# Pinning mixer products behind conditioning visits, and moving the conditioning loads to another queue

## The chip, the cores and the metric

The kernel runs on one NeuronCore of a Trainium2 chip. The metric is device time in microseconds of one execution, as the median of several runs. The engines are named as in the profile: PE is TensorE's matmul, PEld its weight load, DVE is VectorE, ACT is ScalarE, POOL is GpSimd, SP is SyncE, which here only issues DMAs.

## The reference, cut to what matters

One inference step of a decoder layer for 256 prompt tokens and 8 x 4 sample tokens (288 columns in all), width 2048, all in 32-bit floats:

```python
mod = silu(c) @ w_ada + b_ada                       # conditioning: 6 vectors of 2048 for 9 sequences
sh1, sc1, gt1, sh2, sc2, gt2 = split(mod, 6)
xn = rmsnorm(x, g_norm1) * (1 + sc1) + sh1
proj = xn @ w_in                                    # q, k, v, gates of three recurrent branches
y_lru, y_gla, y_ml = rglru(...), gla(...), mlstm(...)   # each also returns its updated state
merged = sum(sigmoid(mg[b]) * (y[b] @ w_br[b]) for b in range(3))
x = x + gt1 * (merged @ w_out)
xn = rmsnorm(x, g_norm2) * (1 + sc2) + sh2
x = x + gt2 * (square(relu(xn @ w_ff1)) @ w_ff2)
y = rmsnorm(x, g_final)
```

The weights are read once: 410 MB come from HBM by the page. The sample group's GLA and mLSTM states (8 and 16 blocks of half a megabyte) are read, updated and written back.

## The kernel before, in words

**The stream.** Activations lie feature-major: 128 partitions by 288 columns for each of 16 tiles of features. `stream` (line 148) multiplies one block of 512 output features: for each group of two k-tiles it loads 512 KB of weights (`raw`, line 155, on SyncE's queue), rounds them to a high part on ScalarE (line 156), takes the low part on VectorE (line 158), and issues 24 matmuls (line 165: high x high, high x low, low x high; four feature tiles, two k-tiles). `raw`, `hi` and `lo` have three buffers each. A block has 8 groups when it sums over 2048 features and 4 when it sums over 1024. After the last group an eviction reads the four PSUM tiles. The order of the blocks is: three q, k, v blocks in two halves of k each (`NPRE = 3`), the fourth of these, two LRU blocks, two GLA gate blocks, the merge of the LRU branch (four times a gate block and a block of `w_br`), two mLSTM input blocks, the GLA merge, two output-gate blocks, the mLSTM merge, `w_out`, then the MLP.

**The steps.** `run` (line 191) drives a block. After each group it does one letter of a pattern set by `every`: `L` starts the next conditioning load, `V` is a visit, `.` nothing. Then it advances each generator in `side` by one step. The generators are the rest of the work, cut into steps by `yield`: the normalisation, `lru`, `gla`, `gates`, `mlstm`. `pace` keeps the last instruction of some kinds: `last` the last matmul of the stream, `hi` and `lo` the last rounding and difference of weights, `prod` the last conditioning product. `skip` in `every` counts the groups before the pattern starts.

**Conditioning.** `w_ada` is 100 MB, and its products have only 9 columns on one side. They are cut into units of at most 1 MB of weights (`units`, `cond_product`). A load puts a unit into a tile given by `raw_tile` from a rotating list of slots that are free at that stage: `None` is the ring tile "ag", a number is one of the big slots, "st" is the pair of tiles that also holds GLA and mLSTM states. A visit multiplies all loaded units (line 269), with the vector as the stationary operand, in strips of 32 columns of the array.

**What sets the order.** A scheduler orders the instructions of every engine by priority and readiness; SyncE alone keeps program order (`manual_schedule`). `issue_after(x)` puts what is traced inside it behind instruction x on x's engine; it is an order, not a wait for the end. Side steps are traced with high priority behind `last`, `lo` and `hi`; a `V` is traced with high priority behind `last`, ahead of the side step of the same group.

**Lines that matter.** `add_slot` (514) adds the second half of a q, k, v block to the first (517) and multiplies by rstd (518). `conv_tile` (587, its taps at 591) and `conv` (593) are the causal convolutions, one or two of eight tiles a step; their sample part runs on GpSimd (601 to 615). In `gla`, `tile_` reads a state tile with the query (1004) and updates it, `head` (1023) scales a head's output, states are loaded at 989 and stored at 1051. In `mlstm`, states are loaded at 1389 (`mC`), read at 1405, updated at 1425 and stored at 1430. Evictions of the merges are at 1099 to 1103. The merges are driven by `merge` (1071).

Of the kernel before, what the change touches and what calls it, by code (L numbers as in the profile page):

```python
# [11 lines left out]
ALU = mybir.AluOpType  # L12
AX = mybir.AxisListType

P = 128
# [6 lines left out]
N = NP + NS  # L22
# [30 lines left out]
def trunk(ctx, tc, io):  # L53
    nc = tc.nc
    PSUM = bass.MemoryType.PSUM
    V, S, G, T, Q = nc.vector, nc.scalar, nc.gpsimd, nc.tensor, nc.sync
# [130 lines left out]
    def every(p, skip=0):  # L187

        pace.update(every=p.split(), n=-skip)

    def run(gen):
        for _ in gen:
            if pace["every"]:
                if pace["n"] >= 0:
                    step(pace["every"][pace["n"] % len(pace["every"])])
                pace["n"] += 1
            for g in list(side):
                with tc.high_priority(), ExitStack() as behind:
                    for e in ("last", "lo", "hi"):
                        behind.enter_context(tc.issue_after(pace[e].ins))  # L200
                    if next(g, side) is side:
                        side.remove(g)
# [4 lines left out]
    def beside(g):  # L207
        side.append(g)
        return g

    def finish(g):

        while g in side:
            if next(g, side) is side:
                side.remove(g)
# [16 lines left out]
        V.transpose(t, ps[:, 256 * h:256 * h + n])  # L232
        return t.rearrange("p (m c) -> p m c", c=32)

    slots = {"ids": (None,), "n": 1}
    halves_of = {}

    def raw_tile():
# [58 lines left out]
    wada = io["wada"]  # L297
# [4 lines left out]
    def ada(kind):  # L302
        def load(raw, k):
            if len(raw) == 2:
                for h in range(2):
                    Q.dma_start(raw[h], wada[kind, h, k])
            else:
                Q.dma_start(raw[0].rearrange("p (h m) -> p h m", h=2), wada[kind, :, k].rearrange("h p m -> p h m"))
        return cond_product(kind, load, 1, 2048, silu_c, ada_finish(kind))

    def ada_half(name, kind, h):

        def load(raw, q):
            Q.dma_start(raw[0].rearrange("p (k m) -> p k m", k=2), wada[kind, h, 2 * q:2 * q + 2].rearrange("k p m -> p k m"))
        return cond_product(name, load, 2, 1024, silu_c, lambda _, pv: ada_finish(kind)(h, pv))

    def shift_product(dst, nb):

        def load(raw, k):
            Q.dma_start(raw[0][:, 0:512 * nb].rearrange("p (b m) -> p b m", b=nb),  # L320
                        io["win"][B_Q:B_Q + nb, k // 2, :, 512 * (k % 2):512 * (k % 2) + 512].rearrange("b p m -> p b m"))

        def add(h, o):
            n = o.shape[1]
            while h and shifts[0] in side:
                yield
            for m in range(n):
                d = dst[h][:, m, 0:NP]
                V.tensor_scalar(d, d, o[:, m, 0:1], None, ALU.add)
                yield  # L330
            d = smp(dst[h])[:, 0:n]
            G.tensor_tensor(out=d, in0=d, in1=o[:, :, 1:9].unsqueeze(3).to_broadcast([P, n, NB, TS]), op=ALU.add)

        def end(h, pv):
            o = sc([P, 8, 9], "cor")[:, 0:pv.shape[1]]
            V.tensor_copy(o, pv[:, :, 0:9])
            shifts.append(beside(add(h, o)))
        return cond_product("cor", load, 1, 512 * nb, lambda k: modf[:, (SH1 * KT + k) * 9:(SH1 * KT + k) * 9 + 32], end)
# [124 lines left out]
    qk, vv = slot(8), slot(9)  # L463
# [50 lines left out]
    def add_slot(dst, base):  # L514
        def f(m, p):
            d = dst[:, base + m, :]
            V.tensor_tensor(out=d, in0=d, in1=p, op=ALU.add)
            V.tensor_tensor(out=d, in0=d, in1=rs, op=ALU.mult)
        return f

    def more_x():
        i = len(xs_)
# [41 lines left out]
    ssq, rs = row("rr"), row("lf")  # L564
# [11 lines left out]
    for h in range(2):  # L576
        for b in range(NPRE):
            ev = (add_slot if h else to_slot)((qk, vv)[b // 2], 4 * (b % 2))
            run(stream(win, B_Q + b, act1, 8 + 8 * h, ev, k0=8 * h, behind=None if h or b else ready))
    finish(pre)  # L580
    every("L L L L . V")
    slots.update(ids=(5, 6, 7, None, 0, 3), n=0)
    rest = beside(last_shifts())
    for b in range(NPRE, 4):
        run(stream(win, B_Q + b, act1, KT, to_slot((qk, vv)[b // 2], 4 * (b % 2))))
# [7 lines left out]
    def conv(x, y, w, b, state, cout, scr, tiles=range(8)):  # L593

        w = w.rearrange("p (k j) -> p k j", k=8)
        f = flat(scr)
        xp = f[:, 0:448].rearrange("p (k b j) -> p k b j", k=8, b=NB)
        acc = f[:, 448:704].rearrange("p (k b t) -> p k b t", k=8, b=NB)
        tmp = f[:, 704:960].rearrange("p (k b t) -> p k b t", k=8, b=NB)
        co = f[:, 960:1176].rearrange("p (k j) -> p k j", k=8)  # L600
        G.dma_start(f[:, 1176:1368], io[state])
        G.tensor_copy(xp[:, :, :, 3:7], smp(x))
        G.tensor_copy(xp[:, :, :, 0:3], f[:, 1176:1368].rearrange("p (k b j) -> p k b j", k=8, b=NB))
        bc = [P, 8, NB, TS]
        for j in range(4):
            wj = w[:, :, j:j + 1].unsqueeze(3).to_broadcast(bc)
            if j == 0:
                G.tensor_tensor(out=acc, in0=xp[:, :, :, 0:4], in1=wj, op=ALU.mult)
                G.tensor_tensor(out=acc, in0=acc, in1=b.unsqueeze(2).unsqueeze(3).to_broadcast(bc), op=ALU.add)
            else:  # L610
                G.tensor_tensor(out=tmp, in0=xp[:, :, :, j:j + 4], in1=wj, op=ALU.mult)
                G.tensor_tensor(out=smp(y) if j == 3 else acc, in0=acc, in1=tmp, op=ALU.add)
        G.tensor_copy(co[:, :, 0:3], x[:, :, NP - 3:NP])
        G.tensor_copy(co[:, :, 3:27].rearrange("p k (b j) -> p k b j", b=NB), xp[:, :, :, 4:7])
        G.dma_start(io[cout], co)
        for m in tiles:
            conv_tile(x, y, w, b, m)
            if len(tiles) < 8 or m not in (0, 3):
                yield


    def lru():
# [101 lines left out]
    with tc.high_priority(), tc.issue_after(pace["prod"].ins):  # L724
        p = misc()
# [110 lines left out]
    def gla():  # L836
# [7 lines left out]
        for h in range(4):  # L844
            p = misc()
# [37 lines left out]
        for t in range(2):  # L883
            for q in range(2):
                p = misc()
# [5 lines left out]
        p = misc()  # L891
# [5 lines left out]
        p = misc()  # L897
# [25 lines left out]
        for t in range(2):  # L923
            p = misc()
# [107 lines left out]
        def do(s, f, *a):  # L1032
            at.setdefault(s, []).append(lambda: f(*a))
# [11 lines left out]
        for h in range(4):  # L1045
            e = 6 * h + (9 if h < 3 else 7)
            do(e, lambda h: gather_tokens(oT, h, pos.pop(h)), h)
            do(e + 1, head, h)
        for n in range(8):
            do(3 + 3 * n, tile_, n)  # L1050
            do(4 + 3 * n, lambda n: S.dma_start(io["o_gla_s"][n], tiles[n][:, 0:1024]), n)
# [19 lines left out]
    def merge(br, y, w):  # L1071
        for b in range(4):
            if br == 0 and b == 2:
                visit()
                slots.update(ids=(None,), n=0)
                every("L . V . . .", skip=5)
            if br == 0:
                gt = acc[b // 2][:, 4 * (b % 2):4 * (b % 2) + 4, :]
            elif br == 1:
                gt = ring.tile([P, 2048], F32, tag="ag", name=nm("ag"))[:, 0:4 * N].rearrange("p (k n) -> p k n", k=4)  # L1080
            else:
                gt = slot(4)[:, 0:4, :]
            run(stream(win, B_MG + 4 * br + b, act1, KT, lambda m, p: S.activation(gt[:, m, :], p, AF.Tanh, scale=0.5)))

            if br == 0 and b == 0:
                for g in (*shifts, lru_):
                    finish(g)
                gla_.append(beside(gla()))
            if br == 1 and b == 0:
                finish(gla_[0])  # L1090
            if br == 2 and b == 0:
                finish(ml_)
                mrg.extend([slot(0, F32R), slot(1, F32R), slot(2, F32R), slot(3, F32R)])

            def ev(m, p):
                k = 4 * b + m
                a = acc[k // 8][:, k % 8, :]
                if br == 0:
                    V.scalar_tensor_tensor(a, gt[:, m, :], 1.0, p, ALU.add, ALU.mult)
                    return  # L1100
                t = t288()
                V.scalar_tensor_tensor(t, gt[:, m, :], 1.0, p, ALU.add, ALU.mult)  # L1102
                (V if br == 1 else G).tensor_tensor(out=a, in0=a, in1=t, op=ALU.add)  # L1103
                if br == 2:
                    h, l = mrg[k // 8][:, k % 8, :], mrg[2 + k // 8][:, k % 8, :]
                    S.activation(h, a, AF.Copy, scale=0.5)
                    V.scalar_tensor_tensor(l, a, 0.5, h.bitcast(F32), ALU.mult, ALU.subtract)

            run(stream(w, b, lambda k: (y[0][:, k, :], y[1][:, k, :]), 8, ev))
# [394 lines left out]

    merge(1, ygla, io["wbg"])
    slots.update(ids=(None, 8), n=0)
    every("L L . V . . .", skip=5)

    mo = slot(3)
    for b in range(2):  # L1510
# [63 lines left out]
    rs = rstd_of(pss)  # L1574
# [190 lines left out]
```

## Time and profile before

| | |
|---|---|
| median of 3 runs | 1971.24 us (1967.84 to 1971.85) |
| the profiled execution | 1971.56 us, its span 1969.5 us |
| PE busy | 1931.1 us, 98% of the span |
| DVE, ACT, POOL busy | 52%, 42%, 10% |
| mean granted clock of TensorE | 0.996 |
| DMA | 429 MB, 218 GB/s on average |

The page has the busy time of the engines, the span in 40 slices, the DMA queues, the chain of waits that ended last, and the costliest groups of instructions. A row of a group reads: line, engine, operation, output tile and input tiles, shapes, count, then busy time and the mean of one in ns, then the engine's idle time ahead of these instructions and what ended it. A row of the timeline reads: start, length, engine, line, operation, tiles, shapes, count, and in brackets the idle time before it with what ended it. A row of the waits reads: who waited for whom, total us, times, longest. Matmul ends are modelled, so the distance between starts says more than the busy time. A conditioning product shows as two records.

### The profile page before, as it was taken

The numbers are of one execution on the slowest core, as the hardware profiler recorded it, in microseconds if no ns is written. First come the engines' busy times: TensorE is split into PE (matmuls) and PEld (weight loads), VectorE is DVE, ScalarE is ACT, GpSimd is POOL, SyncE is SP. The second block draws the span as 40 slices with busy tenths as digits, with TensorE's granted clock in tenths as the row PEclk, the third lists the DMA queues.
The fourth block names the chain that finished last, engine by engine and source line by source line (L and its number), as shares of the span: only waits on it lengthen the run. The fifth ranks groups of instructions, "written<-read, shape, count | busy, mean of one in ns | idle before, by whom it ended". The sixth has DMA issues, their size and how long they took to land.

```text
span 1969.5 us, 35874 instructions
## 1 busy us (share of the span) xinstructions
PE 1931.1 (98%) x15044; PEld 1820.2 (92%) x15044; DVE 1026.1 (52%) x1576; ACT 823.9 (42%) x1179; POOL 206.4 (10%) x279
## 2 busy tenths in 40 slices
PE   6999999999999999999999999999999999999997
PEld 4889889899899999899999899999999999999997
DVE  2573536545674457654445564445444445444565
ACT  3433364435454354343333454443333334343433
POOL 0000100000014010001113331000000000010101
PEclk9999999999999999999999999999999999999999
DMA  9998757547754459967788655644445544444453
GB/s 384 407 342 300 273 207 265 177 139 248 253 169 139 135 186 319 299 248 268 266 290 333 210 192 183 225 161 161 163 162 176 171 164 161 161 162 168 162 173 113
DMA packets 119378, 429.00 MB, mean 218 GB/s; under 512 B 11745, under 2 KB 12033, under 8 KB 119089
## 3 DMA queue, kind: packets, MB, share of 16 engines
q1 hardware_dynamic: 109888, 392.96, 56.4%
q0 software_dynamic: 4576, 16.57, 2.6%
q10 hardware_dynamic: 4752, 17.19, 2.3%
q8 instruction: 118, 1.93, 0.4%
q14 instruction: 44, 0.35, 0.1%
HBM read 409.85 MB, written 16.81 MB: 217 GB/s over the span
## 4 chain that ended last, share of the span: by engine, by line
PE 93%; DMA 4%; DVE 2%; ACT 1%; issue 1%; DVEq 0%; SPq 0%; ACTq 0%; POOLq 0%
PE mm L165 82%; PE pa L269 5%; DMA raw<-win 2%; DVE lo L158 1%; ACT hi L156 0%; DMA s<-mC 0%; DMA s<-wada 0%; DVE s L591 0%; PE px L672 0%; PE px L1422 0%; PE pi L1405 0%; PE px L943 0%; PE px L1336 0%; DMA o_C_s<-s 0%; PE px L1346 0%
## 5 line engine op out<-in xcount | busy, mean ns | idle before, releaser
L158 DVE TENSOR_TENSOR lo<-raw,hi 128x1024 fp32r<-128x1024 f32 x448 | 551.6, 1232 | 595.6 <-ACT hi L156 573.5
L156 ACT ACTIVATE hi<-raw 128x1024 fp32r<-128x1024 f32 x448 | 474.3, 1059 | 797.6 <-PE mm L165 638.5
L165 PE MATMUL mm<-xh,hi 128*128 128x288 f32 x2560 | 757.1, 300 | 5.8 <-ACT xh L493 1.8
L165 PE MATMUL mm<-xl,hi 128*128 128x288 f32 x2560 | 751.3, 296 | 0.0
L165 PE MATMUL mm<-xh,lo 128*128 128x288 f32 x2560 | 733.8, 296 | 3.6 <-DVE lo L158 3.6
L165 PE MATMUL mm<-s,hi 128*128 128x288 f32 x3328 | 660.4, 296 | 0.0
L165 PEld LDWEIGHTS mm<-s,hi 128*128 128x128 f32 x3328 | 529.6, 188 | 5.8 <-issue 5.2
L165 PEld LDWEIGHTS mm<-xh,hi 128*128 128x128 f32 x2560 | 479.7, 188 | 27.6 <-issue 12.8
L165 PEld LDWEIGHTS mm<-xl,hi 128*128 128x128 f32 x2560 | 481.4, 188 | 2.1 <-issue 0.9
L165 PEld LDWEIGHTS mm<-xh,lo 128*128 128x128 f32 x2560 | 474.4, 188 | 7.3 <-DVE lo L158 5.4
L165 PE MATMUL mm<-s,lo 128*128 128x288 f32 x1664 | 477.8, 295 | 0.3 <-DVE lo L158 0.3
L165 PEld LDWEIGHTS mm<-s,lo 128*128 128x128 f32 x1664 | 308.9, 188 | 0.6 <-DVE lo L158 0.5
L158 DVE TENSOR_TENSOR lo<-s,hi 128x1024 fp32r<-128x1024 f32 x80 | 98.0, 1225 | 115.2 <-ACT hi L156 115.2
L156 ACT ACTIVATE hi<-s 128x1024 fp32r<-128x1024 f32 x80 | 84.9, 1061 | 143.2 <-PE mm L165 142.5
L1600 POOL TENSOR_TENSOR t<-t 128x288 f32<-128x288 f32 x64 | 60.2, 951 | 642.9 <-ACT t L1599 642.9
L269 PE MATMUL pa<-s,silc 128*32 128x256 f32 (+1 forms) x624 | 56.1, 452 | 5.6 <-DMA s<-wada 5.6
L1616 DVE TENSOR_TENSOR s<-s,mm 128x288 f32<-128x288 f32 x96 | 40.3, 450 | 33.8 <-PE mm L165 32.6
L269 PEld LDWEIGHTS pa<-s,silc 128*32 128x32 f32 x624 | 19.6, 112 | 26.9 <-issue 12.0
L429 DVE TENSOR_TENSOR s<-t,s 128x288 fp32r<-128x288 f32 x64 | 33.8, 568 | 15.6 <-ACT s L428 15.6
L1103 POOL TENSOR_TENSOR s<-s,t 128x288 f32<-128x288 f32 x16 | 21.0, 1339 | 188.7 <-DVE t L1102 188.7
L428 ACT ACTIVATE s<-t 128x288 fp32r<-128x288 f32 x64 | 28.0, 442 | 24.6 <-POOL t L1600 24.6
L395 POOL TENSOR_TENSOR row<-row,t 128x288 f32<-128x288 f32 x24 | 24.9, 1039 | 112.0 <-ACT t L393 111.0
(396 smaller groups left out, 1054.4 us busy)
## 6 DMA issues: line engine op xcount, KB each, us to landing
raw<-win SPq DMA_DIRECT2D x192, 512.0 KB, 5.0
raw<-wf SPq DMA_DIRECT2D x176, 512.0 KB, 4.2
s<-wada SPq DMA_DIRECT2D x50, 1024.0 KB, 9.3
s<-wf SPq DMA_DIRECT2D x80, 512.0 KB, 3.6
ag<-wada SPq DMA_DIRECT2D x28, 1024.0 KB, 5.9
raw<-wout SPq DMA_DIRECT2D x32, 512.0 KB, 5.7
st<-wada SPq DMA_DIRECT2D x24, 512.0 KB, 7.3
s<-win SPq DMA_DIRECT2D x13, 768.0 KB, 7.1
```

The lines of the kernel that those rows point to most:

```text
L156: pace["hi"] = S.activation(hi, raw, AF.Copy)
L158: pace["lo"] = V.tensor_tensor(out=lo, in0=raw, in1=hi.bitcast(F32), op=ALU.subtract)
L165: pace["last"] = T.matmul(ps, w[:, kk, ms], x, start=k == k0 and i == 0, stop=k == kt - 1 and i == 2)
L269: pace["prod"] = T.matmul(ps[32 * j:32 * j + 32, h * w // 4:(h + 1) * w // 4], stat(k), v[:, j], start=k == 0 and h == 0, stop=k == KT - 1 ...
L395: G.tensor_tensor(out=s, in0=s, in1=sq, op=ALU.add)
L428: S.activation(dst_h[:, r], src[:, r], AF.Copy)
L429: V.tensor_tensor(out=dst_l[:, r], in0=src[:, r], in1=dst_h[:, r].bitcast(F32), op=ALU.subtract)
L1103: (V if br == 1 else G).tensor_tensor(out=a, in0=a, in1=t, op=ALU.add)
L1600: G.tensor_tensor(out=r, in0=r, in1=r, op=ALU.mult)
L1616: V.tensor_tensor(out=a, in0=a, in1=p, op=ALU.add)
```

## The change

Six edits. Mixer steps are also traced behind the last conditioning product. The queue that issues conditioning loads becomes a variable: SyncE's up to the three halved q, k, v blocks, GpSimd's from then on. The multiplication by rstd leaves the eviction and becomes one instruction on four tiles, in a side step. The mLSTM convolution yields after each of its eight tiles. In the GLA, three of the four heads are scaled one step later. After the first gate block of the GLA merge, two units are loaded into the "st" tiles and visited; before the output-gate blocks the pattern is set so that it starts after 11 groups instead of 5 and has one pair of loads in place of two.

```diff
             for g in list(side):
                 with tc.high_priority(), ExitStack() as behind:
-                    for e in ("last", "lo", "hi"):
+                    for e in ("last", "lo", "hi", "prod"):
                         behind.enter_context(tc.issue_after(pace[e].ins))
...
-    slots = {"ids": (None,), "n": 1}
+    slots = {"ids": (None,), "n": 1, "queue": Q}
...
-                    Q.dma_start(raw[h], wada[kind, h, k])
+                    slots["queue"].dma_start(raw[h], wada[kind, h, k])
...
             V.tensor_tensor(out=d, in0=d, in1=p, op=ALU.add)
-            V.tensor_tensor(out=d, in0=d, in1=rs, op=ALU.mult)
         return f
+
+    def by_rstd(dst, base):
+        d = dst[:, base:base + 4, :]
+        V.tensor_tensor(out=d, in0=d, in1=rs.unsqueeze(1).to_broadcast([P, 4, N]), op=ALU.mult)
+        yield
...
             run(stream(win, B_Q + b, act1, 8 + 8 * h, ev, k0=8 * h, behind=None if h or b else ready))
+            if h:
+                beside(by_rstd((qk, vv)[b // 2], 4 * (b % 2)))
     finish(pre)
     every("L L L L . V")
-    slots.update(ids=(5, 6, 7, None, 0, 3), n=0)
+    slots.update(ids=(5, 6, 7, None, 0, 3), n=0, queue=G)
...
             conv_tile(x, y, w, b, m)
-            if len(tiles) < 8 or m not in (0, 3):
-                yield
+            yield
...
-            do(e + 1, head, h)
+            do(e + (2 if h < 3 else 1), head, h)
...
                 finish(gla_[0])
+                slots.update(ids=("st",), n=0)
+                every("L . V . L . V" + 40 * " .")
...
     slots.update(ids=(None, 8), n=0)
-    every("L L . V . . .", skip=5)
+    every("L L . V" + 12 * " .", skip=11)
```

The other loads of conditioning units (the one-tile form of `w_ada`, its half form, and the q, k, v shift products) change their queue in the same way.

More of the change, by code (lines that the diff above doesn't have):

```diff
@@ L305, in load @@
                 for h in range(2):
-                    Q.dma_start(raw[h], wada[kind, h, k])
+                    slots["queue"].dma_start(raw[h], wada[kind, h, k])
             else:
-                Q.dma_start(raw[0].rearrange("p (h m) -> p h m", h=2), wada[kind, :, k].rearrange("h p m -> p h m"))
+                slots["queue"].dma_start(raw[0].rearrange("p (h m) -> p h m", h=2), wada[kind, :, k].rearrange("h p m -> p h m"))
         return cond_product(kind, load, 1, 2048, silu_c, ada_finish(kind))
@@ L313, in load @@
         def load(raw, q):
-            Q.dma_start(raw[0].rearrange("p (k m) -> p k m", k=2), wada[kind, h, 2 * q:2 * q + 2].rearrange("k p m -> p k m"))
+            slots["queue"].dma_start(raw[0].rearrange("p (k m) -> p k m", k=2), wada[kind, h, 2 * q:2 * q + 2].rearrange("k p m -> p k m"))
         return cond_product(name, load, 2, 1024, silu_c, lambda _, pv: ada_finish(kind)(h, pv))
@@ L319, in load @@
         def load(raw, k):
-            Q.dma_start(raw[0][:, 0:512 * nb].rearrange("p (b m) -> p b m", b=nb),
+            slots["queue"].dma_start(raw[0][:, 0:512 * nb].rearrange("p (b m) -> p b m", b=nb),
                         io["win"][B_Q:B_Q + nb, k // 2, :, 512 * (k % 2):512 * (k % 2) + 512].rearrange("b p m -> p b m"))
```

## The prediction

> **What bounds the kernel now.** I read the page first, then TensorE's waits, then the chain of waits in pieces, then timelines around each piece that is no steady run of matmuls.
>
> ```profile
> span 1969.5 us, 35874 instructions
> ...
> PE 1931.1 (98%) x15044; PEld 1820.2 (92%) x15044; DVE 1026.1 (52%) x1576; ACT 823.9 (42%) x1179; POOL 206.4 (10%) x279
> ```
>
> TensorE is the bound: it is busy for 98% of the span, so a shorter load, copy or multiply is worth only what TensorE stops waiting. The profiled execution took 1971.56 us, 2.06 more than its span; the median of the three runs, 1971.24, is 0.32 below it. The sum is made against 1971.56. One steady stretch gives the price of a full matmul (the windows view: stretch, length, busy time and count of each engine, granted clock, DMA share, GB/s):
>
> ```profile
> 1300.00:1900.00 600.00, 600.00 (x4507) 600.00 (x4506) 296.72 (x364) 232.02 (x284) 45.34 (x48) 1.00 0.48 164
> ```
>
> 600 us over 4507 matmuls are 0.133 us each; nothing is to be gained there. What can change lies before 850 us, where the mixer's small products run beside the stream.
>
> **Part 1, the pin behind the visits' products.** A visit is a batch of conditioning products (line 269), strips of 32 columns, four of which can share the array. The chain in pieces (start, length, what, count) has an undisturbed visit at 356; the timeline has one of the same size at 379, cut up by the GLA's transposes (line 887):
>
> ```profile
> 356.36 1.85 PE pa L269 x16
> ```
>
> ```profile
> 374.24 1.03 PE L887 MATMUL px<-con,s 128*128 128x128 f32 x8
> ...
> 379.07 1.04 PE L269 MATMUL pa<-ag,silc 128*32 128x512 f32 x2
> ...
> 380.05 0.33 PE L887 MATMUL px<-con,s 128*128 128x128 f32 x1
> ...
> 388.78 0.38 PE L165 MATMUL mm<-s,lo 128*128 128x288 f32 x1
> ```
>
> Sixteen records take 1.85 us undisturbed. At 379 the same sixteen, with a transpose after each two, take 388.78 - 379.07 = 9.71: every two run alone for about 1 us where they would have shared the array. Eight transposes by themselves took 1.03. Behind one another that is 1.85 + 1.03 = 2.88, so 6.8 us go. The second place is cut by the LRU's gate products (line 672); a whole visit of the same make, 40 records, comes later in the chain:
>
> ```profile
> 249.07 0.97 PE pa L269 x2
> 250.04 0.68 PE px L672 x2
> ...
> 255.95 1.12 PE mm L165 x7
> ```
>
> ```profile
> 288.44 3.58 PE pa L269 x40
> ```
>
> 255.95 - 249.07 = 6.88, against 3.58 + 2 x 0.68 = 4.94 in order (there are two such cuts): 1.9 us go. In both places visit and mixer products are traced in one step of the run loop, the visit first, so the new edge catches the products that cut. I found no third visit that is cut. What the pin adds is an order: a mixer product stands behind a visit that may wait for its load. The visit is already in front of the stream on TensorE's queue, so the stream waits for it as before, and the mixer's readers (ScalarE's copies of the transposes) come sooner than now. **-8.7 us.** The ends are 0, if the products that cut are not caught, and -8.7; more is not there to take, and a loss needs a visit that waits, which belongs to Part 2.
>
> **Part 2, loads on GpSimd's queue.** After the first three q, k, v blocks (at about 140 us) all conditioning loads leave SyncE. SyncE issues in program order and stands at a load until its buffer is free, with the stream's weights behind (SyncE's waits: total, times, longest; then a window, a row of TensorE's timeline and a group of GpSimd):
>
> ```profile
> SPq L308 <- PE pa L269: 88.3, 16, 12.6
> ```
>
> ```profile
> 216.00:228.00 12.00, 11.64 (x115) 8.98 (x117) 7.90 (x24) 4.32 (x8) 3.62 (x8) 1.00 0.17 49
> ```
>
> ```profile
> 237.94 0.40 PE L165 MATMUL mm<-xh,hi 128*128 128x288 f32 x1 [0.95 <-ACT hi L156]
> ```
>
> ```profile
> L989 POOL DMA_DIRECT2D st<-gla x8 | 4.3, 534 | 64.2 <-DMA o_gla_s<-st 59.8 <-PE mm L165 4.5
> ```
>
> SyncE stood 88.3 us before visits, 12.6 at most. One such stop is visible: from 216 to 228 the DMA engines moved 49 GB/s, the weights came late, and TensorE waited 0.95 at 237.94. I take this wait as gone and the other stops as hidden already by the three weight buffers: **-1.0**. Ends: -2.0 (as much again in the small waits around it) and +7 (the state loads of Part 3, whose queue is now shared). An issue costs GpSimd 0.534 us; I count 88 load issues after 140 us and two more because two units now take two tiles each: 90 x 0.534 = 48 us on an engine that is busy for 206 of 1969, hidden by its idle time. Without that cover 0.53 us a load falls on what stands behind it on GpSimd: the convolutions, the GLA and mLSTM state loads, the MLP's squares.
>
> [...]
>
> **Part 3, fewer loads beside the mLSTM states.** Of four units loaded for the output-gate blocks, two move to the start of the GLA merge, into the pair of "st" tiles; the other two keep their buffers ("ag", slot 8) and stand six steps later in the program.
>
> ```profile
> 773.86 0.44 SPq L308 DMA_DIRECT2D ag<-wada  x1
> ```
>
> ```profile
> 775.36 0.53 POOL L1389 DMA_DIRECT2D s<-mC  x1 [8.67 <-DMA o_C_s<-s]
> 779.81 0.53 POOL L1389 DMA_DIRECT2D s<-mC  x1 [3.92 <-DVE st L1425]
> ```
>
> ```profile
> 788.89 1.03 PE L1405 MATMUL pi<-s,s 128*32 128x257 f32 x8 [2.61 <-DMA s<-mC]
> ```
>
> ```profile
> 790.00:792.00 2.00, 2.00 (x9) 2.00 (x10) 0.87 (x2) 0.33 (x1) 0.16 (x1) 0.50 1.04 425
> ```
>
> ```profile
> 146.04 0.54 POOL L601 DMA_DIRECT2D s<-lst  x1 [77.42 <-issue]
> ...
> 224.32 0.44 POOL L602 COPY s<-s 128x256 f32<-128x256 f32 x1 [19.64 <-ACT s L450]
> ```
>
> A first load of 1 MB goes out just before two state loads (a second between them), the last state lands 9 us after its issue, TensorE waits 2.61, and in the 2 us that follow it has half its clock: 1.0 more. If the conditioning loads left, these 3.6 would go. But program order binds SyncE alone. GpSimd's instructions are placed where their buffers are free: the LRU state's load went out at 146.04, 78 us before the copies at 224.32 that follow it in the program. "ag" and slot 8 come free when they do now, so I expect both loads at 772 to 780 again, in the states' own queue. I take **0**, by the rows of before, between -3.6 and +7: both megabytes ahead of both states are 2.1 MB, at half of the 425 GB/s 10 us, of which the states lose about 3 already. The two early units are the same products in two visits instead of one, and DMA is far from full there; nothing is counted. What is late next if a state lands later: the state products (line 1405) stand in TensorE's queue with the stream behind.
>
> **Part 4, one rstd multiply for four tiles.** Twelve multiplies between evictions become three, one step later.
>
> ```profile
> 114.61 0.45 DVE L518 TENSOR_TENSOR s<-s,row 128x288 f32<-128x288 f32 x1
> ...
> 116.44 1.22 DVE L158 TENSOR_TENSOR lo<-raw,hi 128x1024 fp32r<-128x1024 f32 x1
> ```
>
> ```profile
> 117.71 0.40 PE L165 MATMUL mm<-xh,lo 128*128 128x288 f32 x1 [0.98 <-DVE lo L158]
> ```
>
> Three of them stand between 114.61 and 116.44, so the split of the weights starts more than 1 us late, and TensorE waits 0.98 for it: **-1.0**. Ends: -2.0 (the same again at the block before) and +1.4: the new multiply has 4 x 288 = 1152 elements, at the split's 1.22 for 1024 that is 1.4, and it may stand ahead of a split. Those who read these tiles come 90 us later.
>
> **Part 5, three GLA heads one step later.**
>
> ```profile
> 505.68 0.52 DVE L1023 SCALAR_TENSOR_TENSOR s<-s,gn,s 128x288 f32<-128x288 f32 x1
> ...
> 506.90 0.45 DVE L1099 SCALAR_TENSOR_TENSOR s<-s,mm 128x288 f32<-128x288 f32 x1
> ```
>
> ```profile
> 507.50 0.37 PE L165 MATMUL mm<-xh,hi 128*128 128x288 f32 x1 [1.70 <-DVE s L1099]
> ```
>
> A head's three instructions fill 505.68 to 506.90, ahead of a block's last evictions, and TensorE waits 1.70 for the bank. A step later they stand in the next block's first group: **-1.2**; ends -1.7 and +1.2 (the same in front of another eviction).
>
> **Part 6, eight steps for the mLSTM convolution**, where six steps had two tiles twice.
>
> ```profile
> 572.61 8.62 DVE L591 SCALAR_TENSOR_TENSOR s<-s,par,s 128x255 f32<-128x255 f32 x11
> ```
>
> ```profile
> 582.41 0.40 PE L165 MATMUL mm<-xh,lo 128*128 128x288 f32 x1 [1.36 <-DVE lo L158]
> ```
>
> Eleven taps stand in a row, the split is late, TensorE waits 1.36. At 8.62/11 = 0.78 a tap three are 2.35, with a split 3.6 in a step of 24 matmuls, 3.2: the weight buffers carry that for some steps. **-1.0**, ends -1.4 and +0.5. The mLSTM work ends two steps later; its last four steps wait for the output gate anyway, whose 64 steps its 64 now just fill.
>
> **Sum:** -8.7 - 1.0 + 0 - 1.0 - 1.2 - 1.0 = -12.9; 1971.56 - 12.9 = **1958.7 us**.
>
> **The rivals.** *The pin does not bite:* the cutting products are placed by other rules, 1958.7 + 8.7 = 1967.4. Against it is their order in the step. *The states get free:* the conditioning loads land elsewhere, 1958.7 - 3.6 = 1955.1; the load at 146.04 speaks against it. *Slower: GpSimd's queue stands still.* SyncE's stops move to GpSimd, in front of state loads. A state load held there by the mean stop, 88.3/16 = 5.5 us, and needed as tightly as the one of 779.81, costs TensorE 5.5 plus 1.0 of slow clock. Two eat the gain; from three on (19.5) the kernel is slower, at 1958.7 + 19.5 = 1978. For it: GpSimd is in order, and two of its state loads are already short. Against it: a load that is placed when its buffer is free does not stand. [...]
>
> **How the numbers follow.** A measurement of this kernel can tell about 0.2%, 3.9 us, from no change. My sum with its ends, mostly 1953 to 1965: 0.55. States free: 0.15. Pin without bite, some of it below 1967.6: 0.10. Half of the gain given back at new waits, 1965 to 1972: 0.10. Slower: 0.10. So faster 0.80, same 0.09, slower 0.11; 1952 to 1968 leaves out the slow case and some of the two before it.
>
> **What would show it.** Right: the visit near 379 takes 1.9 us with no transpose inside; SyncE no longer waits for visits; GpSimd is busy for about 254 us; the waits at 117, 507 and 582 are gone. Wrong: TensorE waits for states at more places than one, or for a visit's load.

## The result, and the profile after

The changed kernel takes 1962.59 us (median of 6 runs, 1960.51 to 1963.28) against 1970.87 for the kernel before on the same chip (6 runs): a ratio of 0.9960, 95% interval 0.9947 to 0.9973, so 0.4% faster, 8.3 us. The forecast was 1958.7, with 1952 to 1968 as its range. The profiled execution took 1962.52, its span is 1960.7, 8.8 below the span before. Its page:

```profile
span 1960.7 us, 35959 instructions
...
PE 1921.1 (98%) x15060; PEld 1819.7 (93%) x15060; DVE 1028.6 (52%) x1567; ACT 823.7 (42%) x1179; POOL 267.2 (14%) x373
```

TensorE is the bound as before. The pin works: in the chain of waits (start, length, what, count) both visits that were cut are whole, and the products that cut them stand behind.

```profile
244.57 3.58 PE pa L269 x40
248.15 1.17 PE px L677 x4
...
372.21 1.85 PE pa L269 x16
374.06 1.02 PE px L892 x8
```

SyncE's waits for visits are down from 88.3 us (line 308 alone) to those of the first stage, whose loads did not move:

```profile
SPq L314 <- PE pa L269: 8.5, 8, 3.8
```

The timeline of TensorE has three waits that matter. The first is new in size (2.61 before), the other two are new:

```profile
775.07 1.08 PE L1412 MATMUL pi<-st,s 128*32 128x257 f32 x8 [7.62 <-DMA st<-mC]
```

```profile
1029.15 0.50 PE L165 MATMUL mm<-s,hi 128*128 128x288 f32 x2 [0.76 <-DVE rs_t L1545]
...
1031.05 0.40 PE L165 MATMUL mm<-s,lo 128*128 128x288 f32 x1 [0.60 <-DVE lo L158]
```

GpSimd's timeline says why the state at 775 was late, and the view of DMA issues for the moment of 758.37 (queue, count, KB, us to landing) how late:

```profile
755.39 0.53 POOL L1396 DMA_DIRECT2D st<-mC  x1 [7.83 <-DVE s L1110]
755.91 0.71 POOL L308 DMA_DIRECT2D s<-wada  x1
756.62 0.72 POOL L308 DMA_DIRECT2D ag<-wada  x1
758.37 0.56 POOL L1396 DMA_DIRECT2D st<-mC  x1 [1.03 <-DMA o_C_s<-st]
```

```profile
st<-mC POOLq DMA_DIRECT2D x1, 514.0 KB, 16.7
```

The two conditioning loads that the program puts behind the eleventh group of the output-gate blocks went out ahead of a state that TensorE wanted at 767.4; it landed 16.7 us after its issue (9.0 for the late state before). The windows of that time (stretch, length, busy time and count of each engine, clock, DMA share, GB/s) show full DMA engines, and a clock of half for 4 us behind the wait:

```profile
767.00:771.00 4.00, 0.45 (x4) 0.21 (x2) 0.90 (x3) 2.77 (x6) 0.54 (x1) 1.00 1.02 418
771.00:775.00 4.00, 0.00 (x0) 0.00 (x0) 0.00 (x0) 0.00 (x0) 0.53 (x1) 0.63 1.03 408
775.00:779.00 4.00, 3.93 (x21) 3.12 (x22) 2.44 (x6) 0.00 (x0) 0.00 (x0) 0.52 0.17 68
```

A table by stretch carries the rest of this text. A stretch runs from one numbered matmul of the stream (line 165) to another, so that its work in the stream is the same in each kernel; the first column has its times in the kernel before. The other columns are by how many us the stretch is longer or shorter than before, in the profiled executions.

| stretch before | after | pin alone | Parts 4 to 6 alone | Part 2 alone | Part 3 alone | after, two groups on SyncE |
|---|---|---|---|---|---|---|
| 97.4 to 137.0 (Part 4) | -1.3 | 0.0 | -1.3 | 0.0 | 0.0 | -1.3 |
| 194.6 to 268.2 (first cut visit, late weights) | -5.4 | -1.9 | -0.3 | -3.1 | +0.4 | -5.4 |
| 268.2 to 361.4 | -0.1 | +0.5 | +1.3 | -0.1 | +0.8 | -0.1 |
| 361.4 to 400.6 (second cut visit) | -7.0 | -7.0 | 0.0 | 0.0 | 0.0 | -7.0 |
| 475.0 to 507.5 (Part 5) | -1.6 | -1.5 | -1.5 | -1.6 | -1.4 | -1.5 |
| 570.3 to 770.4 (Part 6) | +0.7 | 0.0 | -1.6 | 0.0 | +4.2 | +0.9 |
| 770.4 to 841.5 (output gate, states) | +3.8 | -2.1 | -3.8 | +2.2 | -0.6 | -6.2 |
| 1013.6 to 1070.5 (output projection) | +2.1 | 0.0 | 0.0 | +2.1 | 0.0 | 0.0 |

So 15.6 us were won before 570, and 6.6 of them given back behind it: by the states, at the output projection, and by work that moved into the stretch of 570 to 770.

### The profile page after: what moved, and what is told of

It is laid out like the page before. It is cut to its first block, busy times and chain, and to the rows that moved or that the text cites. A ratio compares the mean times of both kernels' runs of the same rounds, so it can differ in the third digit from the quotient of the medians.

```text
span 1960.7 us, 35959 instructions
## 1 busy us (share of the span) xinstructions
PE 1921.1 (98%) x15060; PEld 1819.7 (93%) x15060; DVE 1028.6 (52%) x1567; ACT 823.7 (42%) x1179; POOL 267.2 (14%) x373
## 4 chain that ended last, share of the span: by engine, by line
PE 93%; DMA 4%; DVE 2%; ACT 1%; issue 0%; DVEq 0%; SPq 0%; ACTq 0%; POOLq 0%
PE mm L165 83%; PE pa L269 4%; DMA raw<-win 2%; DMA st<-mC 1%; DMA raw<-wout 1%; DVE lo L158 1%; DMA s<-wada 0%; ACT hi L156 0%; PE px L677 0%; PE px L1429 0%; PE pi L1412 0%; PE px L948 0%; PE px L1343 0%; DVE s L597 0%; DMA o_C_s<-st 0%
## 5 line engine op out<-in xcount | busy, mean ns | idle before, releaser
L269 PE MATMUL pa<-s,silc 128*32 128x256 f32 (+1 forms) x616 | 49.8, 450 | 5.5 <-DMA s<-wada 5.5
L269 PEld LDWEIGHTS pa<-s,silc 128*32 128x32 f32 x616 | 18.9, 112 | 25.5 <-issue 11.1
L308 POOL DMA_DIRECT2D ag<-wada x23 | 16.5, 719 | 169.7 <-PE pa L269 169.5
```

What stands on the lines that cost most here:

```text
L269: pace["prod"] = T.matmul(ps[32 * j:32 * j + 32, h * w // 4:(h + 1) * w // 4], stat(k), v[:, j], start=k == 0 and h == 0, stop=k == KT - 1 ...
L308: slots["queue"].dma_start(raw[0].rearrange("p (h m) -> p h m", h=2), wada[kind, :, k].rearrange("h p m -> p h m"))
```

## The experiments

**The pin alone**, on the kernel before:

```diff
-                    for e in ("last", "lo", "hi"):
+                    for e in ("last", "lo", "hi", "prod"):
```

> The kernel before with the pin alone: the side work of a step also stands behind the visit's products. The prediction's theory: the two cut visits (249 and 379 us) are whole again, 6.8 + 1.9 = 8.7 us, ratio 0.9956. By the trace of the changed kernel the stretch around 379 is 7.0 shorter and the one around 249 is 4.8 shorter, but the latter holds late weights too (the wait of 0.95 at 237.94 and small ones behind it), which the pin doesn't touch: I expect 7.0 there and 2.0 to 2.5 here, with the waits at 217 to 245 still in place. The rival, that the loads' move and not the pin closed the visits: nothing changes at 379 and the ratio is above 0.998.

Measured: 1961.36 us (before 1971.65), ratio 0.9946 (0.9933 to 0.9958). The visits are whole in this kernel too (chain of waits):

```profile
249.57 3.58 PE pa L269 x40
...
377.86 1.85 PE pa L269 x16
```

7.0 and 1.9 us go in their two stretches, 9.0 in all against 8.7 forecast, with SyncE still standing for visits: the pin closed them, not the move of the loads. Two further gains came with it: the wait at 507 is gone (more on it below), and a state is less late,

```profile
778.49 0.42 PE L1405 MATMUL pi<-s,s 128*32 128x257 f32 x4 [2.09 <-DMA s<-mC]
```

2.09 instead of 2.61, and without a slow clock behind it. The pin alone is about as fast as the whole change.

**Parts 4, 5 and 6 alone**, on the kernel before:

```diff
-            V.tensor_tensor(out=d, in0=d, in1=rs, op=ALU.mult)
+            if h:
+                beside(by_rstd((qk, vv)[b // 2], 4 * (b % 2)))
...
-            if len(tiles) < 8 or m not in (0, 3):
-                yield
+            yield
...
-            do(e + 1, head, h)
+            do(e + (2 if h < 3 else 1), head, h)
```

> The kernel before with Parts 4, 5 and 6 alone (one rstd multiply for four tiles, GLA heads a step later, eight convolution steps). The prediction's prices: 1.0 + 1.2 + 1.0 = 3.2 us, ratio 0.9984; each in its own stretch: the starts of the stream's blocks earlier by 1.0 from 137 us on, by 1.2 more from 507 on, by 1.0 more from 600 on. By the changed kernel's trace the first two are 1.45 and 1.55, the third 1.1 to 1.8 before some of it comes back. The rival, that these gains came from the loads' move (the weights land sooner, so a late split matters less): under 1 us in all.

Measured: 1967.38 us (before 1971.65), ratio 0.9976 (0.9965 to 0.9987): 4.3 us by the medians, where 3.2 were forecast. The executions spread from 1962.9 to 1973.6 and the profiled one is among the shortest, so its stretch of the states (-3.8) is not typical. Part 4 gives 1.3 in its stretch, but the same 1.3 come back between 268 and 361, at a wait of TensorE that the kernel before does not have:

```profile
PE px L851 <- DVE s L754: 1.1, 1, 1.1
```

Such a wait, of 0.3 to 1.1 us, stands in the four kernels with an edit whose early conditioning loads stay on SyncE's queue (the pin alone, Parts 4 to 6 alone, Part 3 alone, all loads on SyncE), and in none with the early loads on GpSimd's. Part 6 gives 1.6 in its own stretch. The stretch of Part 5 is 1.5 shorter, but so it is with the pin, Part 2 or Part 3 alone, which don't have Part 5.

**Part 2 alone**, on the kernel before: all conditioning loads after 140 us on GpSimd's queue, four units still loaded in the output-gate blocks.

```diff
-    slots.update(ids=(5, 6, 7, None, 0, 3), n=0)
+    slots.update(ids=(5, 6, 7, None, 0, 3), n=0, queue=G)
```

> The kernel before with Part 2 alone: conditioning loads on GpSimd's queue from 140 us on, everything else as before, so that four units are still loaded during the output-gate blocks. My theory: the gain before 300 us is that between the last two runs of the other group (all loads on SyncE 1952.9, the early ones on GpSimd 1950.5), 2.4 us, the burst costs 2.1 at the output projection, and up to 4 MB go out in the midst of the states as soon as their buffers are free: a wait of 7 us or more in place of the 2.61 of before. In all 3 to 8 us slower than before, ratio 1.0015 to 1.004. By the prediction's price (1.0 us gained, states unharmed) the ratio is 0.9995.

Measured: 1970.18 us (before 1971.66), ratio 0.9986 (0.9977 to 0.9995). The early gain is 3.1, the burst at the output projection costs 2.1, both about as expected; but I had the states wrong by size. Their wait grows from 2.61 to

```profile
789.89 1.08 PE L1405 MATMUL pi<-s,s 128*32 128x257 f32 x8 [4.48 <-DMA s<-mC]
```

and the stretch by 2.2, not by 7 or more. So the part is slightly faster, not 3 to 8 us slower as I expected.

**Part 3 alone**, on the kernel before, so on SyncE's queue, where program order holds:

```diff
                 finish(gla_[0])
+                slots.update(ids=("st",), n=0)
+                every("L . V . L . V" + 40 * " .")
...
-    every("L L . V . . .", skip=5)
+    every("L L . V" + 12 * " .", skip=11)
```

> The kernel before with Part 3 alone, on SyncE's queue: two of the four units of the output-gate blocks load at the start of the GLA merge, the other two six steps later. On this queue program order holds, so the part does what it says: the wait of 2.61 at 788.89 and the 1.0 of slow clock behind it go, 3.6 us, ratio 0.998. The prediction held that a hoist takes this back; it can't on SyncE. If the two late loads meet later states as closely as the four did the earlier ones, the wait moves and the ratio is 0.9995 or more.

Measured: 1973.93 us (before 1971.66), ratio 1.0008 (0.9996 to 1.0019): no gain, perhaps a loss. The wait of 788.89 is gone and another is there:

```profile
805.40 1.08 PE L1407 MATMUL pi<-st,s 128*32 128x257 f32 x8 [3.54 <-DMA st<-mC]
```

The two early units' visits make the stretch of 570 to 770 longer by 4.2: their products used to run later, and without the pin one of them is cut by the mLSTM's products, two by two as the visits of Part 1 were:

```profile
630.19 0.62 PE L269 MATMUL pa<-st,silc 128*32 128x256 f32 x2
630.74 0.75 PE L1279 MATMUL px<-s,s 128*128 128x288 f32 x2
631.42 0.62 PE L269 MATMUL pa<-st,silc 128*32 128x256 f32 x2
```

**The two loads of the output-gate blocks on SyncE's queue**, on the changed kernel:

```diff
-    slots.update(ids=(None, 8), n=0)
+    slots.update(ids=(None, 8), n=0, queue=Q)
...
-    slots.update(ids=(None, "st", 5), n=0)
+    slots.update(ids=(None, "st", 5), n=0, queue=G)
```

> The changed kernel, with the two conditioning loads of the output-gate blocks ("ag", slot 8) on SyncE's queue instead of GpSimd's; all other loads stay on GpSimd. SyncE issues in program order, so they go out at about 795 us instead of 756. In the changed kernel TensorE waits 7.62 us at 775.07 for an mLSTM state that was issued at 758.37, behind these two loads on the same queue, and then has half its clock for some 3.5 us. My theory (a state stands behind 2 MB of conditioning weights): the wait and the slow clock go, 7.6 + 1.7 = 9.3 us, so 1962.5 - 9.3 = 1953 us, with up to 1.5 us back at a later state, where the states have 6 us of slack. The rival (the DMA engines are simply full between 760 and 775, with whatever traffic): moving 2 MB to 795 moves the wait there, a wait of 3 us or more stands between 795 and 815, and the time is 1957 to 1962.

Measured: 1952.31 us (before 1969.24), ratio 0.9913 (0.9900 to 0.9927). In its trace TensorE waits for no state. They went out at 781 and 787, not at 795 as I had expected. The state issued at 759.18 landed in

```profile
st<-mC POOLq DMA_DIRECT2D x1, 514.0 KB, 7.5
```

This one row of the program costs the changed kernel 10 us. The run doesn't yet say whether by the queue or by the time, since both differ; the next three do.

**The same two loads on ScalarE's queue**, at the same time as in the changed kernel, every other instruction in the order it had (the diff is that of the run above with `queue=S`).

> The changed kernel, with the same two loads on ScalarE's queue; they are issued at the same time as in the changed kernel (about 756 us), and every other instruction stands where it stood. Only the queue differs. The queue theory: the state issued at 758.37 no longer has 2 MB ahead of it on its own queue, it lands in 7 to 10 us instead of 16.65, the wait of 7.62 at 775.07 shrinks to under 2.5, and the time is 1953 to 1957. The bandwidth theory: the same bytes go over the same engines in the same microseconds, the state lands later than 13 us after its issue, the wait stays above 4 us and the time is 1959 to 1963.

Measured: 1959.01 us (before 1969.24), ratio 0.9942 (0.9929 to 0.9954). DMA issues for the state's moment, and TensorE's timeline:

```profile
st<-mC POOLq DMA_DIRECT2D x1, 514.0 KB, 10.8
```

```profile
766.48 0.64 PE L1412 MATMUL pi<-st,s 128*32 128x257 f32 x8 [0.64 <-DMA st<-mC]
...
770.27 0.64 PE L1412 MATMUL pi<-st,s 128*32 128x257 f32 x8 [2.18 <-DMA st<-mC]
...
782.10 0.64 PE L1412 MATMUL pi<-s,s 128*32 128x257 f32 x8 [1.14 <-DMA s<-mC]
```

Neither theory has it alone: the wait lies in the range of the queue theory, the time in that of the bandwidth theory, the landing between the two. With the same two megabytes in flight, but on another queue, the state lands in 10.8 instead of 16.7 us, and the wait falls from 7.62 to 2.18: so some 6 us of its delay are the bytes ahead of it on its own queue. The other 3 (10.8 against 7.5 with the loads elsewhere in time) I put down to the traffic of all queues together, 416 GB/s at a DMA share of 1.02 in the 3.0 us up to 770.27, against 286 GB/s at 0.95 from 765 to 770 with the loads on SyncE's; that is an estimate, no run holds it apart. Two other states now wait 0.64 and 1.14. The time fell by 3.6 us of the 10.

The changed kernel's trace shows the line itself. The loads' packets on GpSimd's queue have 4096 bytes, a state's 4112. The loads' 512 packets start from 759.0 to 772.7; between 761.03 and 769.66 no packet of a state starts on that queue, although one was issued at 758.37. So the state's delay is not in its issue: it stood behind the two loads.

**The two loads later, still on GpSimd's queue:** a one-column copy by VectorE into each buffer, which reads the last tile of the first output-gate block.

```diff
-                raw = raw_tile()
+                raw = raw_tile(); 'late' in slots and V.tensor_copy(raw[0][:, 0:1], slots['late'][:, 3, 0:1])
...
-    mo = slot(3)
+    mo = slots['late'] = slot(3)
```

> The changed kernel, with the two loads still on GpSimd's queue, but each behind a one-column copy by VectorE into its buffer that reads the last tile of the first output-gate block: they can't go out before about 797 us. Only the time differs, not the queue. If the harm is that they go out where the states are tight (758 to 776), the wait of 7.62 goes and the time is 1953 to 1956. If the harm is the shared queue wherever it happens, the last states (issued at 785 to 800) stand behind them, a wait of 3 to 8 us comes between 800 and 815, and the time is 1957 to 1963.

Measured: 1962.12 us (before 1969.24), ratio 0.9956 (0.9943 to 0.9968), as slow as the changed kernel. The loads went out at 789.73, not at 797 as I had expected, but still ahead of the last states. GpSimd's timeline, the landing of its last state, and TensorE:

```profile
789.73 0.71 POOL L308 DMA_DIRECT2D ag<-wada  x1
790.44 0.72 POOL L308 DMA_DIRECT2D s<-wada  x1
794.53 0.58 POOL L1396 DMA_DIRECT2D s<-mC  x1 [3.37 <-PE px L1429]
```

```profile
s<-mC POOLq DMA_DIRECT2D x1, 514.0 KB, 16.3
```

```profile
810.84 1.09 PE L1412 MATMUL pi<-s,s 128*32 128x257 f32 x8 [6.36 <-DMA s<-mC]
```

The wait of 775 is gone, and the last state has it instead: 16.3 us behind the same two megabytes. It is not the one place among the states that hurts but the queue: a state that followed the two loads on it cost TensorE a wait of 7.62 us in the one place and of 6.36 in the other.

**One of the two on each queue:** "ag" on SyncE's, slot 8 on GpSimd's.

> The changed kernel, with one of the two loads of the output-gate blocks ("ag") on SyncE's queue and the other (slot 8) left on GpSimd's, where it goes out at about 755 us, just ahead of the state of 758. One megabyte stands ahead of the state instead of two. By the queue theory the state's delay follows the bytes ahead of it: with none the wait was 0, with two loads 7.62 us; the state's 16.65 us from issue to landing becomes about 11 to 12, so that it lands 2 us after it is wanted or just in time: a wait of 0 to 3 us and a time of 1952 to 1957. If the wait has another cause than the bytes ahead (a fixed price of GpSimd's queue for any load between two states), 5 us or more stay and the time is 1958 or more.

Measured: 1958.73 us (before 1971.66), ratio 0.9933 (0.9920 to 0.9947), 1.7 above the range that I gave and within that of the other theory, which also asked for a wait of 5 us or more; the wait is 2.13. The state behind one megabyte:

```profile
st<-mC POOLq DMA_DIRECT2D x1, 514.0 KB, 11.1
```

```profile
770.38 0.82 PE L1412 MATMUL pi<-st,s 128*32 128x257 f32 x8 [2.13 <-DMA st<-mC]
```

The series of landings is 7.5, 11.1 and 16.7 us with none, one and two megabytes ahead: 3.6 for the first and 5.6 for the second, each from one profiled execution. The delay grows with the bytes; by the run on ScalarE's queue, some two thirds of the 9.2 in all are the queue's.

**The last stage's loads back on SyncE**, on the changed kernel:

```diff
-    slots.update(ids=(None, "st", 8, 9, "xh", "xh", "xl", "xl", "xh", "xh", None, "st", 8, 9), n=0)
+    slots.update(ids=(None, "st", 8, 9, "xh", "xh", "xl", "xl", "xh", "xh", None, "st", 8, 9), n=0, queue=Q)
```

> The changed kernel, with the conditioning loads of the last stage (the output projection and the MLP) back on SyncE's queue. In the changed kernel GpSimd sends about 10 of them between 987 and 1005, the DMA engines are full (418 GB/s from 1000 to 1020), the weights of the output projection land late and TensorE waits 0.92 at 1029.15 and 0.77 at 1031.04. My theory (a burst that program order on SyncE used to spread): both waits go, 2.1 us between the starts of its second and fourth block, so 1960.4. The rival: SyncE stops for the visits there again and gives the same back, 1962 to 1963.

Measured: 1962.06 us (before 1969.24), ratio 0.9960 (0.9946 to 0.9974). The medians can't tell it from the changed kernel (1962.59), and 1962.06 lies in the range that I gave the rival; the profiled execution is 2.1 shorter (1960.41), and just in the stretch of the output projection, where both waits are gone. Windows of the changed kernel show what was there, ScalarE's timeline who waited first:

```profile
1000.00:1010.00 10.00, 10.00 (x78) 10.00 (x77) 7.15 (x11) 4.17 (x8) 5.48 (x6) 1.00 1.02 418
1010.00:1020.00 10.00, 10.00 (x76) 9.83 (x76) 2.64 (x3) 2.33 (x3) 0.00 (x0) 1.00 1.02 418
```

```profile
1017.23 1.06 ACT L156 ACTIVATE hi<-raw 128x1024 fp32r<-128x1024 f32 x1 [6.22 <-DMA raw<-wout]
```

GpSimd sent nine loads, 8 MB, between 987 and 1005, as buffers came free; on SyncE they stand between the weights. That SyncE's stops give nothing back shows only in the next run, where the medians gain 1.8 us with this edit (1952.31 to 1950.48).

**Both groups back on SyncE**, the two edits together:

> The changed kernel with both groups back on SyncE: the two loads of the output-gate blocks and the loads of the last stage; the loads from 140 us to the GLA merge and those of the mLSTM merge stay on GpSimd. If the two harms are independent: 1952.3 - 2.1 = 1950.2 us. If SyncE's stops in the last stage cost what the burst did: 1952 or more.

Measured: 1950.48 us (1949.49 to 1950.94; before 1971.65), ratio 0.9890 (0.9877 to 0.9904): the fastest kernel here with the next one, 12 us below the changed kernel. The two harms add up (TensorE's waits for states in this trace):

```profile
PE pi L1412 <- DMA s<-mC: 0.3, 1, 0.3
```

**The same without Part 3**, four units again in the output-gate blocks:

> The kernel with both groups back on SyncE (1950.5), with Part 3 undone: four units load during the output-gate blocks again, the first two from the sixth step, and none at the start of the GLA merge. It prices Part 3 where the queue does what the program says. If Part 3 does what it says there, the wait for a state behind the early pair comes back: 2.6 of wait and 1.0 of slow clock, 1954.1 us. If it is worth nothing even there (as it was on the kernel before, ratio 1.0008, where the wait only moved to a later state): 1950.5, with a wait at one state or another that differs from one execution to the next.

Measured: 1950.81 us (before 1969.32), ratio 0.9901 (0.9884 to 0.9917). Part 3 is worth nothing: the state behind the early pair waits

```profile
764.87 0.64 PE L1412 MATMUL pi<-st,s 128*32 128x257 f32 x8 [1.46 <-DMA st<-mC]
```

and what its absence costs between 770 and 841 (3.0 us: this wait, and a visit of 1.9 that now stands there) it saves between 570 and 770, where no early units run (2.6 us less than with Part 3).

**All loads on SyncE**, the changed kernel without its `queue=G`:

> The changed kernel with no load on GpSimd's queue: all conditioning loads stay on SyncE, in the new program order; the other five parts stay. What it loses is the gain of Part 2, what it loses of harm is the state behind 2 MB (wait of 7.62 at 775) and the burst before 1029. The prediction's price of Part 2 is 1.0 us; by the traces the stretch from 195 to 268 is 5.4 us shorter in the changed kernel, of which the cut visit is 2.0 to 2.5, so 2.9 to 3.4 would be Part 2. From the changed kernel with two loads on SyncE (1952.3) and the burst's 2.1: at a price of 1.0 it takes 1952.3 - 2.1 + 1.0 = 1951.2, at 3.2 it takes 1953.4. The rival, that a load on GpSimd's queue is worth more all over (SyncE's 88 us of stops): 1956 or more.

Measured: 1952.92 us (before 1971.65), ratio 0.9910 (0.9894 to 0.9926). Against 1950.48 that prices Part 2, with its two harms left out, at 2.4 us. The profiled execution took 1958.61, the three others 1952.6 to 1953.1, so its trace holds waits that the others can't all have had. One of them is that of Part 5 (VectorE, then TensorE):

```profile
495.38 0.51 DVE L1028 SCALAR_TENSOR_TENSOR s<-s,gn,s 128x288 f32<-128x288 f32 x1
...
496.61 0.45 DVE L1106 SCALAR_TENSOR_TENSOR s<-s,mm 128x288 f32<-128x288 f32 x1
```

```profile
497.21 0.37 PE L165 MATMUL mm<-xh,hi 128*128 128x288 f32 x1 [1.77 <-DVE s L1106]
```

Part 5 is in this kernel, and the head (lines 1028, 809, 1028) stands in front of the block's eviction, between the same instructions as before.

## Why the prediction was right, and where not

The direction and the range held, the size less: -12.9 forecast, -9.0 in the profiled execution. The missing 4 us are a sum of errors of both signs. By the table, 7.6 us went the wrong way against the forecast (3.8 at the states, 2.1 at the output projection, 1.7 between 570 and 770), and some 3.5 the right way (2.5 of them between 194.6 and 268.2). That these offset each other, and brought the total closer than its terms, is luck.

**Part 1 was right**, in mechanism and size: -8.7 forecast, -9.0 measured alone, at the two places named.

**Part 2 was right in mechanism and mis-sized twice.** Its early gain is 2.4 (medians) to 3.1 (its stretch), not 1.0: I counted the one wait of 0.95 that the page named and took the small ones around it for an end of the range. Missing from the step is the last stage. I named the queues and their order in the middle of the kernel, but not that a load without program order goes out in a burst as buffers come free; that costs 2.1 between 1013 and 1070. GpSimd is busy for 267.2 us, not 254: the mean issue of a whole megabyte takes 0.72 us, not the 0.534 of the half megabyte that I took as its price (groups of instructions):

```profile
L308 POOL DMA_DIRECT2D ag<-wada x23 | 16.5, 719 | 169.7 <-PE pa L269 169.5
...
L1396 POOL DMA_DIRECT2D st<-mC x8 | 4.3, 534 | 76.1 <-DMA o_C_s<-st 27.6 <-DVE s L1434 14.1 <-DVE st L1432 12.2
```

**Part 3 is the step that failed.** The hoist was foreseen (loads at 772 to 780 in the states' own queue; they went at 756), and so was its price, as an end: +7. The term itself was taken as 0. A wait of 7.62 with some 1.8 of slow clock took the place of one of 2.61 with 1.0, about 6 us more, near that end. What the choice of 0 missed is that before, the two megabytes were on another queue than the state: the rows showed the same bytes in the same microseconds, and I took that for the same delay. The runs have 10.8 us on another queue, 16.7 on the same. Where the loads obey, Part 3 is worth 0 indeed, but for another reason than the hoist: 1950.48 with it, 1950.81 without. The two early units, for which nothing was counted, take 2.6 us between 570 and 770; a visit of 1.9 leaves the output-gate blocks for it.

**Part 4** -1.0 forecast, -1.3 measured; the wait at 117.71 is smaller, not gone (0.60 at 116.24 after), and so is the one at the block before, which I had counted as an end only (0.93 at 99.28, then 0.36 at 98.58). On SyncE's queue the 1.3 come back at 343, as said above. **Part 6** -1.0 forecast, -1.6 measured in its stretch; its wait is halved (0.66 at 565.61, so 0.7 of the 1.6; the rest isn't traced to a wait), and Part 3's early units hide the gain in the changed kernel (+0.7 in that stretch). **Part 5** -1.2 forecast, -1.6 measured at the place, and it is not Part 5: the wait of 1.70 goes in three kernels without that part, and is there, 1.77, in one that has all parts but the GpSimd queue (in an execution longer than its others). The step that failed read a move in the program as a move on VectorE; in the changed kernel too the head stands in front of the eviction:

```profile
490.14 0.51 DVE L1028 SCALAR_TENSOR_TENSOR s<-s,gn,s 128x288 f32<-128x288 f32 x1
```

```profile
491.96 0.37 PE L165 MATMUL mm<-xh,hi 128*128 128x288 f32 x1
```

There it begins 1.8 us before TensorE asks for the bank; before, it began 0.1 us before that (505.68 against 507.50 - 1.70). What shifts the one against the other is late weights. In the kernel before, ScalarE waits for a group of them (timeline); from the next split (503.75) on, the state update, the head and the eviction follow in a row on VectorE:

```profile
500.12 1.06 ACT L156 ACTIVATE hi<-raw 128x1024 fp32r<-128x1024 f32 x1 [4.35 <-DMA raw<-win]
```

These weights were issued at 491.46, right behind a conditioning load on SyncE's queue (490.97), and landed after 8.6 us. With all loads on SyncE, where the wait of 1.77 stands, the same group landed after 9.1 us. In the kernels with the pin, Part 3 or Parts 4 to 6 alone it stands behind the same load, but landed after 6.9 to 7.1 us, and the wait is gone; with the loads on GpSimd's queue no conditioning load stands before it. So Part 2 alone is enough for the 1.6 of the changed kernel, and Part 5 is not shown to add to them. Why the group lands sooner in the three kernels that keep its place isn't settled.

**The rivals.** *The pin does not bite* fell with the first experiment. *The states get free* did not happen in the changed kernel; its time, 1955, is bettered by 1952.31 once the two loads leave the queue. *GpSimd's queue stands still* was half right: GpSimd stood 170 us for visits at line 308, with "ag" alone, but no mLSTM state load was: those waited mostly for stores and for VectorE (the row of line 1396 above), and the two conditioning loads among them went out with no idle time ahead (755.91 and 756.62). What held a state was the two loads already issued, and one state paid, not three.

## What to carry to other kernels

In these runs a queue was two things, an order of issue (in the kernel before, SyncE stood 88.3 us for visits at line 308) and a line of bytes (a state landed in 16.7 us behind two megabytes on its queue, in 10.8 with them on another). Moving bulk loads off an in-order issuer freed the issuer (2.4 us here), but on a queue that also carries small loads with a deadline the first megabyte ahead made those land 3.6 us later and the second 5.6; give the deadline loads a queue without bulk (1959.01 us here, against 1962.59), or keep the bulk where program order paces it (1952.31). And a move in the program was a move on an engine only where order and not readiness placed the instruction (the head of Part 5 still went at 490.14, in front of the eviction): look for the moved instructions in the new trace before you credit them with a gain.

## What the runs showed of the hardware that was not expected

The clock behind a wait was not a matter of the wait's length alone. TensorE waited 2.18 us at 770.27 with the loads on ScalarE's queue, and 2.13 at 770.38 with one on each queue. The windows behind the two, first the one, then the other:

```profile
770.27:771.77 1.50, 1.50 (x15) 1.08 (x16) 0.74 (x3) 0.00 (x0) 0.00 (x0) 1.00 0.90 367
771.77:773.27 1.50, 1.50 (x13) 1.50 (x12) 1.50 (x3) 0.00 (x0) 0.00 (x0) 1.00 0.28 115
```

```profile
770.38:771.88 1.50, 1.50 (x11) 0.91 (x12) 0.36 (x2) 0.30 (x1) 0.00 (x0) 0.61 1.08 279
771.88:773.38 1.50, 1.50 (x8) 1.50 (x7) 0.22 (x1) 0.00 (x0) 0.53 (x1) 0.50 0.96 336
```

Nor was it the work in the 3.0 us before the wait's end, of which TensorE was busy for 0.82 and 0.87 us. Behind the longer wait, of 2.18, the granted clock stayed at 1.00; behind the shorter it was 0.61, 0.50 and 0.75 in three stretches of 1.5 us. The pin alone kept 1.00 after 2.09, the kernel before had 0.54 and 0.50 after 2.61, and behind each longer wait for a state (3.54 us with Part 3 alone, 4.48 with Part 2 alone, 6.36 with the two loads later, 7.1 with the last stage's loads back on SyncE, 7.62 in the changed kernel) the clock was 0.50 for the first 1.5 us. So a wait of 2.13 was enough once, and one of 2.18 did no harm; what decides between them these runs don't show.
